# A token mixer with expert retrieval: the expert choice in finer steps, a block's last LayerNorm moved into the choice's empty steps

## The chip, the cores and the metric

The kernel runs on one core of one Trainium2 chip. Its time is the device time of one execution in microseconds (us). Five engines work side by side: TensorE (PE, matrix products), VectorE (DVE), ScalarE (ACT), GpSimd (POOL) and SyncE (SP), which only issues transfers. Each runs its own instructions strictly in order and waits for the others by semaphores.

## The reference

One layer over 128 context tokens and 512 latent tokens, 640 rows of 2048 float32 values. A token mixer (state-space scan, short convolution, Conformer convolution, gates) comes first, then the part that matters here, a retrieval among 16384 one-neuron experts:

- queries `q = h @ w_q` in 8 heads of two halves; each half is scored against 128 keys
- the 16 best of the 128 scores in each of the 16 columns (8 heads, two halves), then the 16 best of the 256 sums of pairs in each head: 128 experts for a token, with softmax weights `g`
- `out = sum over chosen experts k of g_k * gelu(x . u_k) * v_k`
- `y = LN(2 ** 0.25 * x1 + gate * out) * ln2_g + ln2_b`

## The kernel before

The 640 rows are five blocks of 128 tokens, taken in the order 3, 4, 2, 1, 0. Mixer, queries and scores of all blocks are done by 2530 us; the choice of the first block is done on the way. Then `experts` (L1374) runs to the end, half of the time.

**A block's experts.** For a block the union of its chosen experts is a list. `chunk` (L1265) treats 256 of its entries (134 chunks in all five blocks): GpSimd gathers the rows of `u` and `v` and of the weights (`ur`, `vr`, `gr`), PE transposes `u` (`turn`), ScalarE takes its high part `wh` and VectorE the low part `wl`, PE makes three products for each (`up`), then `weigh` and `down` add to four PSUM banks `acc`. 24 chunks (`K0`) are written out for each block, the few more stand behind conditions. `chunk` is a generator: it yields nine times, one yield a step. The first step holds two turns, the second `weigh`, and the third to eighth a turn each.

**What is dealt into the steps.** `choose` (L1034) for the next block is a generator too, and the caller asks it for one piece in every step. Its pieces, before the change:

- the 16 columns, two in a step (8 steps); the sums of pairs (2); the 8 heads, one in a step (8); splitting the places (1); one-hot sums that look up the experts' numbers (12); softmax (2): 33 steps
- a loop over n from 0 to 33 that makes the weights of all 16384 experts by one-hot products of four tokens on PE, two steps each for 32 of them. ScalarE copies a product into the staging tile `Gs`, which has one buffer; at n = 9, 17, 25 and 33 it is full and SP stores its 2 MB to `G_d`, in runs of 32 values. Four steps of counting on VectorE follow each time, and 20 empty steps behind the first three
- the list of the chosen experts: counts (1 step), 16 rounds of maximum and replacement, four in a step (4), places and reads of the first entries on GpSimd (9)

`finish` (L1302) of the block before, for blocks 1 to 3 of the order beside the choice, for block 4 alone: in chunk 0 it loads the rows of `x` and the gate and multiplies the four banks (`fy`); from chunk 1 on one piece in every second step: four of update and statistics, the square root, the row loads (`row`, L1339, four buffers), four of two updates each that take two LayerNorm rows of 512 values, and the store of the output. The last block's finish runs behind all chunks.

**The order of the work.** `pin` (L1359) ties every engine's instructions of one block's written-out part to the order in which they are written, SP's transfers too. SP issues ahead of the other engines as far as buffers are free.

Of the kernel before, what the change touches and what calls it, by code (L numbers as in the profile page):

```python
# [151 lines left out]
class Kern:  # L152
# [871 lines left out]
                self.nc.vector.scalar_tensor_tensor(x[:, s], x[:, s], a, g, op0=o0, op1=o1)  # L1024

    def top16(self, vals, idx, src):
        v = self.nc.vector
        v.max(vals[:, 0:8], src)
        v.max_index(idx[:, 0:8], vals[:, 0:8], src)
        v.match_replace(src, vals[:, 0:8], src, -3.0e38)  # L1030
        v.max(vals[:, 8:16], src)
        v.max_index(idx[:, 8:16], vals[:, 8:16], src)

    def choose(self, b, S=None):  # L1034
# [8 lines left out]
        IX = T.tile([128, 16, 16], U32, name="IX", tag="IX", bufs=1)  # L1043
        for c in range(16):
            self.top16(V[:, c], IX[:, c], S[:, c])
            if c % 2:
                yield
        IF = T.tile([128, 16, 16], F32, name="IF", tag="IF", bufs=1)
        v.tensor_copy(IF, IX)
        sh = [128, 8, 16, 16]  # L1050
# [3 lines left out]
        cand = T.tile(sh, F32, name="cand", tag="Gs", bufs=1)  # L1054
# [4 lines left out]
        TV = T.tile([128, 8, 16], F32, name="TV", tag="TV", bufs=1)  # L1059
        SE = T.tile([128, 8, 16], U32, name="SE", tag="SE", bufs=1)  # L1060
        for h in range(8):
            self.top16(TV[:, h], SE[:, h], cand[:, h].rearrange("p a b -> p (a b)"))
            yield

        I12 = T.tile([128, 3, 128], F32, name="I12", tag="I12", bufs=1)
# [30 lines left out]
        p = ps.tile([128, 3, 128], F32, name="g", tag="m", bufs=1)  # L1096
# [5 lines left out]
        for n in range(34):  # L1102
            if full is not None:
                n1, p = full
                if n1 % 8 == 0:
                    st = T.tile([128, 128, 32], F32, name="Gs", tag="Gs", bufs=1)
                nc.scalar.copy(st[:, :, n1 % 8 * 4:n1 % 8 * 4 + 4], p.rearrange("j t i -> j i t"))
                if n1 % 8 == 7:
                    nc.sync.dma_start(self.G_d[b][:NE].rearrange("(i j) t -> j i t", j=128)
                                      [:, :, n1 // 8 * 32:n1 // 8 * 32 + 32], st)  # L1110
            full = None
            if ready is not None:
                n1, oh, dd = ready
                p = ps.tile([128, 4, 128], F32, name="g", tag="m", bufs=1)
                for j in range(4):
                    nc.tensor.matmul(p[:, j], oh[:, j], dd[:, j], start=True, stop=True)  # L1116
                full = n1, p
            ready = None
            if n < 32:
                oh = T.tile([128, 4, 128], F32, name="oh", tag="oa", bufs=2)  # L1120
                dd = T.tile([128, 4, 128], F32, name="dd", tag="od", bufs=2)
                for j in range(4):
                    k1, k2, w = (it[:, i, n * 4 + j:n * 4 + j + 1] for i in range(3))
                    v.tensor_scalar(oh[:, j], self.iota, k2, None, op0=ALU.is_equal)
                    v.tensor_scalar(dd[:, j], self.iota, k1, w, op0=ALU.is_equal, op1=ALU.mult)
                    if j == 1:
                        yield
                ready = n, oh, dd
            yield
            if n % 8 == 1 and n > 1:  # L1130
                for q in range(4):
                    v.tensor_reduce(cnt[:, n // 8 - 1, q * 32:q * 32 + 32], st[:, q * 32:q * 32 + 32], axis=AX.X,
                                    op=ALU.add)
                    yield

                for _ in range(20 if n < 32 else 0):
                    yield

        f = T.tile([128, 128], F32, name="f", tag="f", bufs=1)
        v.tensor_reduce(f, cnt.rearrange("p q i -> p i q"), axis=AX.X, op=ALU.add)  # L1140
# [7 lines left out]
        for r in range(16):  # L1148
            s = slice(r * 8, r * 8 + 8)
            v.max(L[:, s], f)  # L1150
            if r < 15:
                v.match_replace(f, L[:, s], f, 0.0)
            if r % 4 == 3:
                yield
        li = T.tile([128, 128], I32, name="li", tag="li", bufs=1)
        v.tensor_scalar(li, L, -1.0, None, op0=ALU.add)
# [19 lines left out]
        p = ps.tile([128, 128], F32, name="g", tag="m", bufs=1)  # L1176
# [4 lines left out]
        p = ps.tile([128, 128], F32, name="g", tag="m", bufs=1)  # L1181
# [4 lines left out]
        p = ps.tile([128, 128], F32, name="g", tag="m", bufs=1)  # L1186
# [187 lines left out]
    def experts(self):  # L1374
        nc, tc = self.nc, self.tc
        E = self.E = self.pool("experts")
        one = lambda shape, name, dt=F32: E.tile(shape, dt, name=name)
        self.vr = [one([128, D], "vr%d" % j) for j in range(2)]
        self.y = one([128, D], "fy")
        self.t = one([128, CH], "t")  # L1380
        self.gr, self.w = one([128, 2, 128], "gr"), one([128, 2, 128], "w")
        self.ur = [[one([128, D], "ur%d%d" % (c, j)) for j in range(2)] for c in range(2)]
        hb = self.H[GB]
        self.xs = [[t[:, j] for t in hb] for j in range(2)]
        first = [one([128, D], "uf%d" % j) for j in range(2)]
        pieces = [[t[:, k * 512:k * 512 + 512]
                   for t in [self.wp.tile([128, 1024], F32R, name=n, tag=n, bufs=self.hl_bufs) for _ in range(3)]
                   for k in range(2)] for n in ("wh", "wl")]
        self.uh, self.ul = ([t.rearrange("p (k e) -> p k e", k=2) for t in p[:4]] for p in pieces)
        self.rr, self.nrow = [t.bitcast(F32) for p in pieces for t in p[4:]], 0  # L1390
        self.fx = [self.wp.tile([128, 1024], F32, name="wr", tag="wr", bufs=self.raw_bufs) for _ in range(2)]
        ps = self.pool("ps5", space=PSUM)
        self.acc = ps.tile([128, 4, 512], F32, name="acc")
        self.tb = [ps.tile([128, 512], F32, name="tb%d" % j) for j in range(2)]
        self.a = ps.tile([128, CH], F32, name="a")
        pending, rows, fin = None, None, iter(())
        mark = self.pin()
        self.load_x(0)
        for j in range(2):
            self.gather_u(self.order[0], 0, j)  # L1400
        for i, b in enumerate(self.order):
            more = self.choose(self.order[i + 1]) if i < 4 else iter(())
            for c in range(K0):
                if c == 0 and i:
                    fin = self.finish(i - 1)
                    next(fin)
                for n, _ in enumerate(self.chunk(i, c, pending, rows)):
                    next(more, None)
                    if c and n % 2:
                        next(fin, None)  # L1410
                if c == 0:
                    next(fin, None)
                rows, pending = None, (c == 0, self.xs[i % 2])
                if c == 0 and i < 4:
                    self.load_x(i + 1)
            for _ in more:
                pass
            if i < 4:
                rows = first
                for j in range(2):  # L1420
                    self.gather_u(self.order[i + 1], 0, j, first[j])
            n = nc.values_load(self.lists[b]["count"][0:1, 2:3].bitcast(I32), min_val=0, max_val=NE,
                               skip_runtime_bounds_check_because="it counts the ones among 16384 flags")
            self.pin(mark)
            pending = False, self.xs[i % 2]
            with contextlib.ExitStack() as st:  # L1426
                for c in range(K0, NCH):
                    st.enter_context(tc.If(n > c * CH, name="more%d_%d" % (i, c)))
                    mark = self.pin()
                    for _ in self.chunk(i, c, pending):  # L1430
                        pass
                    self.pin(mark)
            mark = self.pin()
        self.nbank = 1
        self.up(7, pending[1])
        self.weigh()
        for u in range(8):
            self.down(u, False)
        for _ in self.finish(4):
            pass  # L1440
        self.pin(mark)
        self.close(ps, E)
# [95 lines left out]
```

## Time and profile before

| | |
|---|---|
| median of three runs | 5276.44 us (5272.74 to 5280.17) |
| the profiled execution | 5268.44 us, its span 5266.7 us |
| PE busy | 4800.3 us, 91% of the span |
| VectorE busy | 2879.7 us, 55% |
| ScalarE, GpSimd busy | 1599.6 and 1601.8 us, 30% each |
| mean granted TensorE clock | 0.961 of full speed |
| moved by DMA | 1085 MB, mean 206 GB/s |

A share of busy time is a mean over stages with different limits, so the rows further below are cut by chunk: a chunk's limits are taken where VectorE's product of `weigh` (`w<-tb,gr`) starts, in its second step. SP issued a store at 3320.68 and the list `L_d` of the same block at 3514.48 us, two times that the text uses. A granted clock of 1.00 is the upper of TensorE's two levels, and a mean between the levels says how long it was at the lower one.

### The profile page before, as it was taken

What the parts mean: (1) busy time and instruction counts of PE and PEld (TensorE: products, weight loads), DVE (VectorE), ACT (ScalarE), POOL (GpSimd) and SP (SyncE); (2) the same over time, 40 slices, a digit from 0 to 9 for tenths busy, and PEclk for the clock granted to TensorE, in tenths of its full rate; (3) what the DMA queues carried; (4) which work ended last, traced back from release to release, by engine and by line L of the source; (5) the groups of instructions that cost most, each with busy time, mean ns of one, the idle gap of its engine ahead of it and who ended that gap; (6) DMA issues with size and microseconds to landing.
All of it is one profiled execution on the core that took longest, in us unless ns stands there. A gap on an engine that the chain in (4) does not pass through costs nothing. (4 is left out here: it accounts for less than half of the span.)

```text
span 5266.7 us, 74372 instructions
## 1 busy us (share of the span) xinstructions
PE 4800.3 (91%) x29015; PEld 3989.4 (76%) x29015; DVE 2879.7 (55%) x6240; ACT 1599.6 (30%) x2561; POOL 1601.8 (30%) x1628
## 2 busy tenths in 40 slices
PE   8999989999999997969699979997999889989997
PEld 3799879999999977759577657765677667767775
DVE  6693593466534544781555566555655484634333
ACT  3324424433223123323133223322332223323222
POOL 2000493000000004534243434343334434344442
PEclk8999989999999998989799999999999999999998
DMA  6544336554325465563578768776777668867765
GB/s 238 195 173 144 126 129 213 192 173 172 114 98 165 147 214 200 158 153 136 187 242 257 233 221 272 244 235 240 254 242 243 255 218 267 247 231 290 260 250 212
DMA packets 576711, 1085.00 MB, mean 206 GB/s; under 512 B 375643, under 2 KB 388955, under 8 KB 501819
## 3 DMA queue, kind: packets, MB, share of 16 engines
q0 software_dynamic: 97712, 596.41, 30.5%
q1 hardware_dynamic: 460394, 429.32, 27.4%
q10 hardware_dynamic: 18208, 54.08, 2.6%
q8 instruction: 239, 3.92, 0.3%
q14 instruction: 158, 1.29, 0.1%
HBM read 967.53 MB, written 112.13 MB: 205 GB/s over the span
## 5 line engine op out<-in xcount | busy, mean ns | idle before, releaser
L1241 DVE TENSOR_TENSOR wl<-tb,wh 128x512 fp32r<-128x512 f32 x1072 | 738.0, 690 | 1368.1 <-ACT wh L1240 1366.7
L1240 ACT CAST wh<-tb 128x512 fp32r<-128x512 f32 x1072 | 627.5, 585 | 1873.2 <-PE tb L1239 1776.6
L1262 PE MATMUL acc<-vr,w 128*128 128x512 f32 x2144 | 1096.8, 604 | 30.3 <-DVE w L1257 30.1
L1248 PE MATMUL a<-wh,hh 128*128 128x256 f32 x2144 | 966.9, 451 | 1.8 <-PEq L1426 1.8
L1239 PE MATMUL tb<-cst,ur 128*128 128x128 f32 x4160 | 649.6, 279 | 68.1 <-DMA ur<-in_pu,ix 58.1
L1248 PE MATMUL a<-wl,hh 128*128 128x256 f32 x2144 | 618.8, 289 | 48.9 <-DVE wl L1241 48.7
L193 ACT CAST wh<-wr 128x1024 fp32r<-128x1024 f32 x339 | 355.5, 1050 | 983.4 <-PE a L630 380.4
L1248 PE MATMUL a<-wh,hl 128*128 128x256 f32 x2144 | 614.2, 286 | 0.0
L1248 PEld LDWEIGHTS a<-wl,hh 128*128 128x128 f32 x2144 | 419.9, 196 | 255.3 <-issue 170.5
L1239 PEld LDWEIGHTS tb<-cst,ur 128*128 128x128 f32 x4160 | 493.1, 143 | 150.9 <-issue 75.8
L1248 PEld LDWEIGHTS a<-wh,hh 128*128 128x128 f32 x2144 | 420.4, 196 | 199.4 <-issue 189.7
L630 PE MATMUL a<-h,wl 128*128 128x320 f32 x2368 | 550.9, 313 | 19.4 <-DVE wl L194 19.4
L1204 POOL DMA_INDIRECT vr<-in_pv,ix x268 | 256.1, 955 | 1015.5 <-PE acc L1262 909.8
L194 DVE TENSOR_TENSOR wl<-wr,wh 128x1024 fp32r<-128x1024 f32 x281 | 343.8, 1225 | 380.3 <-ACT wh L193 373.6
L630 PE MATMUL a<-h,wh 128*128 128x320 f32 x2368 | 549.0, 313 | 0.0
L630 PE MATMUL a<-l,wh 128*128 128x320 f32 x2368 | 545.9, 312 | 0.0
L1262 PEld LDWEIGHTS acc<-vr,w 128*128 128x128 f32 x2144 | 341.4, 194 | 103.9 <-issue 69.2
L630 PEld LDWEIGHTS a<-h,wl 128*128 128x128 f32 x2368 | 400.9, 190 | 21.7 <-DVE wl L194 21.0
L1248 PEld LDWEIGHTS a<-wh,hl 128*128 128x128 f32 x2144 | 416.2, 194 | 0.0
L630 PEld LDWEIGHTS a<-h,wh 128*128 128x128 f32 x2368 | 405.6, 190 | 12.0
L630 PEld LDWEIGHTS a<-l,wh 128*128 128x128 f32 x2368 | 400.9, 190 | 0.8
L1204 POOL DMA_INDIRECT gr<-G_d,ix x268 | 265.9, 992 | 365.4 <-DVE w L1257 280.9
(396 smaller groups left out, 7450.0 us busy)
## 6 DMA issues: line engine op xcount, KB each, us to landing
wr<-in_wmod SPq DMA_DIRECT2D x152, 512.0 KB
wr<-in_win SPq DMA_DIRECT2D x83, 512.0 KB
G_d<-Gs SPq DMA_DIRECT2D x20, 2048.0 KB
wrx<-in_win SPq DMA_DIRECT2D x69, 512.0 KB
wrx<-in_wmod SPq DMA_DIRECT2D x40, 512.0 KB
wr<-in_wo SPq DMA_DIRECT2D x36, 512.0 KB
wr<-in_wq SPq DMA_DIRECT2D x32, 512.0 KB
wrx<-in_wq SPq DMA_DIRECT2D x32, 512.0 KB
```

The lines of the kernel that those rows point to most:

```text
L193: nc.scalar.copy(h, raw)
L194: (eng or nc.vector).tensor_sub(l, raw, h.bitcast(F32))
L630: nc.tensor.matmul(a, w, x[:, kt, c0:c0 + n], start=kt == 0 and i == 0, stop=kt == nk - 1 and i == 2)
L1204: self.nc.gpsimd.indirect_dma_start(out=out, out_offset=None, in_=table, in_offset=bass.IndirectOffsetOnAxis(ap=idx, axis=0))
L1239: nc.tensor.transpose(p[:, k, j * 128:j * 128 + 128], rows[j][:, kt * 128:(kt + 1) * 128], self.ident)
L1240: nc.scalar.copy(self.uh[g % 4], p)
L1241: nc.vector.tensor_sub(self.ul[g % 4], p, self.uh[g % 4].bitcast(F32))
L1248: self.nc.tensor.matmul(self.a, a[:, kt], w[:, k], start=kt + n == 0, stop=kt == 15 and n == 2)
L1262: self.nc.tensor.matmul(self.acc[:, d], self.w[:, j], self.vr[j][:, d * 512:d * 512 + 512], start=first and j == 0, stop=j == 1, skip_grou ...
```

## The change

`top16` is cut in two behind its replacement (`top16_steps`). The choice yields behind each column (16 steps for 8), twice in a head (16 for 8), and behind two rounds of the list in place of four (8 for 4). The empty steps behind a store are 13 in place of 20 and say so by yielding `"idle"`. The caller asks the finish for a piece only in a step in which the choice is idle or over, and no more in every second step; what might be left of it is drawn behind the chunks.

```diff
     def top16(self, vals, idx, src):
+        for _ in self.top16_steps(vals, idx, src):
+            pass
+
+    def top16_steps(self, vals, idx, src):
         v = self.nc.vector
         v.max(vals[:, 0:8], src)
         v.max_index(idx[:, 0:8], vals[:, 0:8], src)
         v.match_replace(src, vals[:, 0:8], src, -3.0e38)
+        yield
         v.max(vals[:, 8:16], src)
         v.max_index(idx[:, 8:16], vals[:, 8:16], src)
...
         for c in range(16):
             self.top16(V[:, c], IX[:, c], S[:, c])
-            if c % 2:
-                yield
+            yield
...
         for h in range(8):
-            self.top16(TV[:, h], SE[:, h], cand[:, h].rearrange("p a b -> p (a b)"))
+            yield from self.top16_steps(TV[:, h], SE[:, h], cand[:, h].rearrange("p a b -> p (a b)"))
             yield
...
-                for _ in range(20 if n < 32 else 0):
-                    yield
+                for _ in range(13 if n < 32 else 0):
+                    yield "idle"
...
-            if r % 4 == 3:
+            if r % 2:
                 yield
...
                 for n, _ in enumerate(self.chunk(i, c, pending, rows)):
-                    next(more, None)
-                    if c and n % 2:
+                    if next(more, "idle") == "idle" and c:
                         next(fin, None)
...
             for _ in more:
+                pass
+            for _ in fin:
                 pass
```

## Rows read from the trace of the kernel before

**Rows 1.** Busy us (instructions) by chunk: second block, ten undisturbed chunks.
```profile
core 0: us, PE busy (x) PEld busy (x) DVE busy (x) ACT busy (x) POOL busy (x), PEclk, DMA share, GB/s
3096.30:3130.30 34.00, 19.31 (x93) 13.27 (x94) 32.03 (x129) 4.48 (x8) 7.91 (x9) 0.90 0.55 196
3130.30:3160.30 30.00, 21.07 (x98) 14.48 (x97) 28.73 (x85) 6.35 (x10) 8.02 (x8) 0.84 0.44 152
3160.30:3182.00 21.70, 19.73 (x107) 14.73 (x106) 19.40 (x31) 6.34 (x11) 9.91 (x8) 0.89 0.55 178
3182.00:3203.30 21.30, 19.88 (x113) 14.84 (x111) 16.25 (x38) 8.65 (x14) 9.00 (x8) 0.93 0.90 322
...
3492.40:3514.60 22.20, 16.73 (x94) 12.22 (x95) 20.70 (x66) 4.79 (x9) 7.61 (x8) 0.96 1.14 321
3514.60:3535.30 20.70, 20.36 (x112) 15.60 (x111) 7.52 (x19) 5.40 (x11) 7.80 (x9) 0.88 0.48 164
3535.30:3557.40 22.10, 18.22 (x99) 13.92 (x98) 5.82 (x11) 5.07 (x9) 13.12 (x14) 0.92 0.59 223
...
4820.20:4990.20 170.00, 166.53 (x980) 123.99 (x980) 58.41 (x90) 50.66 (x90) 76.01 (x80) 1.00 0.69 255
```

**Rows 2.** The same: first block's chunks 0 to 3, last block's 1 to 3.
```profile
2561.50:2597.60 36.10, 20.11 (x88) 17.71 (x88) 33.70 (x142) 6.95 (x12) 1.26 (x2) 0.59 0.37 140
2597.60:2622.20 24.60, 19.21 (x100) 13.66 (x99) 23.46 (x77) 5.07 (x9) 7.60 (x8) 0.92 0.46 160
2622.20:2641.80 19.60, 18.94 (x105) 13.87 (x103) 16.15 (x19) 5.34 (x10) 9.35 (x8) 0.92 0.51 175
2641.80:2661.90 20.10, 18.40 (x111) 14.12 (x111) 13.70 (x34) 8.37 (x14) 8.81 (x8) 1.00 0.71 251
4750.40:4803.00 52.60, 50.64 (x300) 37.64 (x298) 29.15 (x52) 17.76 (x30) 23.60 (x24) 1.00 0.91 325
```

**Rows 3.** VectorE groups, chunk 0: count | busy us, mean ns | idle.
```profile
L1241 DVE TENSOR_TENSOR wl<-tb,wh 128x512 fp32r<-128x512 f32 x8 | 5.3, 674 | 0.0
...
L1030 DVE MATCH_REPLACE8 S<-V,S 128x128 f32<-128x128 f32 x14 | 3.9, 276 | 0.0
L1056 DVE TENSOR_TENSOR cand<-V 128x1024 f32<-128x1024 f32 x2 | 2.4, 1216 | 0.0
L1317 DVE TENSOR_TENSOR fy<-acc,wh 128x512 f32<-128x512 f32 x2 | 1.4, 683 | 0.0
L1030 DVE MATCH_VALUE_LOAD S<-V,S 128x8 f32 x14 | 1.3, 92 | 0.5
```

**Rows 4.** VectorE groups, chunk 1: a head's replacement.
```profile
L1030 DVE MATCH_REPLACE8 cand<-TV,cand 128x256 f32<-128x256 f32 x8 | 3.3, 408 | 0.0
```

**Rows 5.** GpSimd's timeline at the choice's end: start us, us, [idle before <-releaser].
```profile
3532.61 0.94 POOL L1204 DMA_INDIRECT vr<-in_pv,ix  x1 [5.93 <-PE acc L1262]
...
3547.68 0.95 POOL L1204 DMA_INDIRECT ur<-in_pu,ix  x1 [0.30 <-issue]
```

**Rows 6.** PE's waits from 3535.3 to 3557.4: us in total, times, longest.
```profile
PE tb L1239 <- DMA ur<-in_pu,ix: 3.9, 1, 3.9
```

**Rows 7.** SP's DMA queue (packets, MB), 2865 to 2893 and 3348 to 3354.5.
```profile
q1 hardware_dynamic: 16400, 2.10, 56.6%
...
q1 hardware_dynamic: 128, 0.02, 1.7%
```

**Rows 8.** Timelines: a store's issue on SP, ScalarE's next copy into `Gs`.
```profile
2865.00 0.36 SPq L1109 DMA_DIRECT2D G_d<-Gs  x1
...
2915.70 0.59 ACT L1107 COPY Gs<-g 128x512 f32<-128x512 f32 x1
```

**Rows 9.** DMA packets by size, 3514.6 to 3518.5, and 3518.5 to 3519.2.
```profile
DMA packets 313, 0.99 MB, mean 255 GB/s; under 512 B 65, under 2 KB 185, under 8 KB 214
...
DMA packets 33, 0.02 MB, mean 25 GB/s; under 512 B 22, under 2 KB 30, under 8 KB 33
```

**Rows 10.** SP's DMA queue, 3126 to 3133.4, four LayerNorm rows.
```profile
q1 hardware_dynamic: 576, 1.05, 49.5%
```

## The prediction, made before the changed kernel was run

> **What bounds the kernel now.** All that changes lies in the last stage, the experts: five blocks of 24 written-out chunks, nine steps each, with the choice for the next block and the finish of the last one dealt into those steps. I read first the busy time by chunk. Ten chunks without such work take 170.0 us, 17.0 each or 1.89 a step, with PE busy for 166.5 [rows 1]: there TensorE is the bound, with VectorE at 58.4, 5.84 a chunk. In the first two chunks of a block it is otherwise: 34.0 and 30.0 us, VectorE busy for 32.0 and 28.7, PE for 19 and 21 at a granted clock of 0.90 and 0.84 [rows 1]. The next two take 21.7 and 21.3, and three at the end of the choice 22.2, 20.7 and 22.1. The first block has no finish: 36.1, 24.6, 19.6, 20.1 [rows 2]. The chunks between carry the choice's one-hot products on PE; these are spread as before, and I count them as unchanged. Then I read VectorE's groups for the price of each step, GpSimd's timeline for the end of the choice, and the DMA queue for the store.
>
> **The choice's first part.** A column of the choice is five instructions of about 0.28 us and three loads of 0.09: 1.70 us [rows 3]. Before, two come in a step (3.4 us beside one low part, `wl`, of 0.67), after, one (2.4). A head is five of about 0.42 and three loads: 2.36 us [rows 4]; after, its steps hold 1.45 and 0.91. Counted from the second step of a chunk to that of the next, chunk 0 of a block has now 14 columns (23.8), the two sums of pairs with a cast (2.7), four products of the finish (2.7) [rows 3] and the chunk's own 5.84: 35.0, read 34.0, so neighbours overlap by 3%. After, it has 9 columns, 15.3 + 2.7 + 5.84 = 23.8, less 3%: 23.1. Chunk 1 has 6 columns, the sums and half a head, 10.2 + 2.7 + 1.45 + 5.84 = 20.2, less 3%: 19.6. Chunks 2 to 4 hold nine half heads or nine one-hot steps, which work on as many elements as the sums of pairs, 1.2 [rows 3]: some 10.5 + 5.84 = 16.3 at most: under PE's 17.0. What began in chunk 3 (softmax, first products) moves to chunk 5; without a finish beside it, it costs 3.1 over 17.0 [rows 2].
>
> Two engines that are both nearly full don't hide each other wholly: the first block's chunk 2 had 16.2 of VectorE and took 19.6, of which 8% is the clock (0.92, 1.6 us) and 1.0 is left [rows 2]. I add 0.5, 1.0, 0.7, 0.5 and 1.3 for chunks 0 to 4, 4.0 in all; the ends are none and 2.6 each, 13 a block. Over 17.0 the first chunks of blocks 1 to 3 cost 17.0 + 13.0 + 4.7 + 4.3 = 39.0 before and 6.1 + 2.6 + 4.0 + 3.1 = 15.8 after: 23 us saved in each, three times, 69. The first block saves 36.1 - 23.2 = 12.9 in chunk 0 (ten columns by the same count, clock 0.59 now), 24.6 - 20.6 = 4.0 in chunk 1, 1.9 in chunk 2, less 1.8 in chunks 3 and 4: 17.
>
> **The list's rounds.** Sixteen rounds of a maximum, a load and a replacement, three of a column's instructions on as many elements: 0.28 + 0.09 + 0.28 = 0.65 each [rows 3]. Four a step are 2.6 + 0.67 = 3.3 against PE's 1.89; two are 2.0. Four steps lose 1.4 each before, eight 0.1 after: 4.8 less. The next chunk's granted clock is 0.88 [rows 1], 2.5 us of 20.7; I count half of it back. 6 us a block, four blocks: 24; the ends are 2 and 9 a block.
>
> **Where the choice ends.** It has 189 steps now: 33 up to the products, 66 + 16 + 60 in them, 14 behind. After: 49, 66 + 16 + 39, 18: 188. So the six list reads on GpSimd come one step earlier, ahead of the chunk's last gather of `vr`. That gather waits for PE until 3532.61, the six come behind it, and by that `ur` for the next chunk but one is issued at 3547.68 [rows 5]; PE waits 3.9 for it [rows 6], in a chunk at clock 0.92. With the six in GpSimd's idle time before that gather, about 4 us of the backlog goes, and `vr` is not needed for half a chunk. 4 us a block, four blocks: 16; the ends are 0 (the reads are held by their own inputs) and 5.1, the chunk's whole excess.
>
> **The empty steps behind a store.** The staging tile has one buffer. A store's first overwriting copy came 26 steps after its issue, 2865.00 to 2915.70, 1.95 us a step [rows 8]; after the change 19 steps, some 37 us. That store's packets were all through within 28 us; the slowest, issued at 3320.68, had 128 of them behind 3348 and the last before 3354.5, at most 34 us [rows 7]. So the copy, behind which ScalarE's high parts are queued and for these PE, doesn't wait: 0, with 3 us to spare in the worst case.
>
> **The finish in the first empty stretch.** It leaves chunks 1 to 3 (counted above) and begins in the sixth step behind the first store: statistics in four steps, the square root, the row loads, four updates. Each of the eight adds two instructions of some 0.68, as the products of the finish take [rows 3], to one low part: 2.0 against 1.89. In block 4, where the finish runs alone in every second step, three chunks took 52.6, 1.6 over [rows 2]. In every step I take 2.5, three blocks: 7.5 lost, and 1.5 lost in block 4, which now deals it into consecutive steps; the ends are 0 and 5 each.
>
> Its LayerNorm rows are the new wait. In SP's order they now follow the store, and their first pair is wanted by VectorE twelve steps behind it, at 23.4 us. Do they pass the store? The list `L_d`, issued at 3514.48 while the fourth store was under way, shows it: 120 packets of 512 B to 2 KB by 3518.5, and the other 8 only then, with the store's last ones [rows 9]. So on each ring they stay behind: at 28 us, plus about a quarter of the 7.4 in which four such rows came [rows 10], less what runs on ahead on the other rings: I take 28.7. VectorE then stands for 5.3 us with the low parts queued behind the update, and PE has one step of work: 5.3 + 2.0 - 1.9 = 5.4, and about 2.1 for the clock (0.84 to 0.92 in starved chunks). 7.5 a block, three blocks: 22.5 lost; the ends are 0 and 14 each (a late ring, 34 us).
>
> The Trainium skill, in "DMA: Bandwidth & Descriptors", section "Queues, rings and completion order", speaks against this move: on each SDMA engine descriptors are consumed in ring order, and SP has one ring on each. By that rule the 22.5 are paid, and the trace agrees in the 8 late packets of the list; were rows free to pass the store, as on an idle queue, the sum would be 117 saved in place of 94.5.
>
> **Sum.** 17 + 69 + 24 + 16 - 7.5 - 1.5 - 22.5 = 94.5 us saved. The profiled execution took 5268.4, so 5174; the median of the three runs, 5276.4, is 8 above it, which gives 5182.
>
> **The rivals.** (a) The rows don't cost their wait: they land before 23.4 because most rings are early, or VectorE runs late by itself. For it: most of a store's packets go early; against it, an instruction needs all 128 packets. 5182 - 22.5 = 5160. (b) The evening out gives less: coupling at twice my 4.0 (16 us more over four blocks), the list reads held by their inputs (16), and a late ring in all three first stores (18): 5232. For it speaks chunk 2 of the first block, against it that the chunk started behind a full VectorE. (c) Slower than before: with 19 steps the store is not through, and ScalarE stands at twelve copies (three in each of four blocks). It decides from some 38.5 us on, 37 and one step of slack; to undo 94.5 each copy must stand 8 us, and with a store of 49 each stands 10.5: 5182 + 126 = 5308. Against it is the slowest store read, 34 us; for it only that gathers come denser once chunks are shorter. That the finish is not dealt as written can't well be: every empty step asks for it, and 11 pieces fit into 13.
>
> **Chances.** The forecast 0.52, (a) 0.20, (b) 0.22, (c) 0.06, of which 0.05 is slower. The range goes from 5140, (a) with no coupling at all (16 less) and a little more, to 5232, (b). A change under 0.2% (some 10 us, what a measurement of this kernel can tell) needs (b) and half of (c): 0.03. Faster 0.92.
>
> **What would show it.** Chunks 0 and 1 of blocks 1 to 3 at about 23.6 and 20.6 us, chunks 2 to 4 at 17 to 18.5; the chunk with the rounds at 17 to 18; no PE wait for `ur` near the end of the choice; a VectorE wait of some 5 us for a row of `in_lnr` in three blocks, once each; no wait of the staging copy for the store there. I am wrong if chunks 0 and 1 stay over 26 with VectorE not busy, if the copy waits for the store, or if the row wait is absent or above 12.

## The result: 79.8 us saved, 14.7 less than forecast

The changed kernel took 5195.95 us, the median of four runs (5186.60 to 5200.09), against 5275.76 for the kernel before on the same chip (5272.74 to 5280.17): a ratio of 0.9846, 95% interval 0.9829 to 0.9863. Forecast was 5182, in a range from 5140 to 5232. Its profiled execution took 5195.74 (span 5193.9), 72.7 below the profiled one of before. The medians lie 79.8 apart, since the one profiled before was 7.3 under the median beside which it stands here, the one after at it.

Busy time by chunk in the second block, cut as in [rows 1] (columns as there): chunks 0 to 2, then 7 to 9, then 19 and 21; the last row is the first block's chunk 0.

```profile
3071.60:3095.30 23.70, 18.81 (x96) 14.17 (x97) 21.77 (x85) 4.48 (x8) 8.55 (x9) 0.87 0.81 277
3095.30:3115.40 20.10, 18.92 (x102) 13.89 (x100) 18.53 (x67) 5.31 (x10) 7.80 (x8) 0.90 0.44 152
3115.40:3133.20 17.80, 16.96 (x98) 12.44 (x98) 15.01 (x45) 4.86 (x10) 7.61 (x8) 1.00 0.74 238
3211.70:3232.00 20.30, 19.60 (x124) 15.07 (x123) 14.92 (x34) 6.37 (x12) 7.65 (x8) 1.00 0.99 239
3232.00:3261.80 29.80, 16.96 (x95) 12.88 (x96) 15.82 (x31) 7.36 (x12) 7.85 (x8) 0.85 0.99 309
3261.80:3282.40 20.60, 19.38 (x119) 15.14 (x119) 11.91 (x33) 6.53 (x12) 7.94 (x8) 0.97 0.92 316
3459.30:3477.80 18.50, 16.69 (x98) 12.45 (x98) 14.93 (x58) 4.63 (x9) 7.60 (x8) 1.00 1.05 325
3495.80:3513.80 18.00, 16.88 (x100) 12.35 (x98) 5.83 (x10) 5.07 (x9) 10.45 (x11) 1.00 0.76 266
2566.40:2589.70 23.30, 15.06 (x91) 13.31 (x91) 21.77 (x91) 6.94 (x12) 1.03 (x2) 0.87 0.44 172
```

Chunks 0 and 1, 34.0 and 30.0 before [rows 1], take 23.7 and 20.1; the first block's chunk 0 falls from 36.1 [rows 2] to 23.3. Chunk 19, with the list's rounds, falls from 22.2 to 18.5 and VectorE's share of it from 20.7 to 14.9 us; chunk 21 takes 18.0, from 22.1. One chunk is new, 29.8 us with no engine busy for more than 17: the first one behind a store.

The waits in that chunk (in total, times, longest), and SP's own timeline there (start, duration):

```profile
PE tb L1260 <- DVE wl L1245: 12.4, 1, 12.4
...
DVE wr L1335 <- DMA wh<-in_lnr: 5.8, 1, 5.8
DVE wr L1336 <- DMA wl<-in_lnr: 3.9, 1, 3.9
...
DVE wr L1335 <- DMA wl<-in_lnr: 2.4, 1, 2.4
```

```profile
3218.86 0.37 SPq L1113 DMA_DIRECT2D G_d<-Gs  x1
3219.33 26.50 SPq L1348 DMA_DIRECT2D wh<-in_lnr  x1
3246.27 1.82 SPq L1348 DMA_DIRECT2D wl<-in_lnr  x2
3248.18 2.89 SPq L1348 DMA_DIRECT2D wh<-in_lnr  x2
```

VectorE stands three times for LayerNorm rows, 12.1 us together, with a low part queued behind; `weigh`'s transposes on PE wait 12.4 us for that, from 3247.6 to 3260.0. The granted clock falls to a mean of 0.85: some 9 of the 29.8 us at the lower level, 1.2 GHz. Most of these pass while PE stands; it worked at that level for only 3.2 us behind the wait:

```profile
3252.90:3260.00 7.10, 0.00 (x0) 0.00 (x0) 2.97 (x5) 0.00 (x0) 0.00 (x0) 0.50 0.76 295
3260.00:3263.20 3.20, 3.17 (x13) 2.96 (x14) 2.95 (x5) 0.33 (x1) 0.67 (x1) 0.50 0.91 219
```

The first row's issue alone stood 26.50 us on SP behind the store, until 3245.8; the others were issued only then. The store's packets ended at 3248.9. In the next two blocks the issue stood 22.95 and 22.47 us, and the chunk took 29.3 and 27.8.

One table shows where the time went. It sums the time of each chunk (from one start of `weigh`'s product to the next) over 17.0 us, by block in the order of work and by part of the choice: the first part (chunks 0 to 2 before, 0 to 4 after), the one-hot products (to chunk 18), the list (19 to 22), the rest of the block. Blocks are counted from one here and below; the prediction counts them from zero. Each pair is before, after:

| | first part | products | list | end of the block |
|---|---|---|---|---|
| 1st block | 29.3, 11.5 | 38.3, 39.3 | 13.8, 3.1 | 11.4, 9.2 |
| 2nd | 34.6, 12.9 | 38.5, 51.9 | 14.0, 3.5 | 11.6, 11.6 |
| 3rd | 34.0, 11.9 | 38.7, 53.0 | 13.5, 3.4 | 11.2, 9.0 |
| 4th | 34.0, 11.8 | 38.6, 54.1 | 13.9, 3.7 | 9.3, 11.5 |

The first part saves 83.8, the list 41.5, the products give back 44.2. The last block, which has no choice, loses 5.0, of which 2.6 in its first chunk. The stages ahead of the experts, which the change doesn't touch, took 4.9 us longer in this execution. In the traces of the eight runs below they took from nothing to 6 us longer than in the trace of before, so this is the spread from one execution to the next.

In the fourth block a third store, issued at 4432.0, was under way for 39.9 us instead of the 24.0 to 32.5 of the other stores beside the choice, and ScalarE's copy waited for it, the only such wait beside the experts in this trace:

```profile
ACT Gs L1111 <- DMA G_d<-Gs: 4.6, 1, 4.6
```

### The profile page after: what moved, and what is told of

Read it like the earlier page. It is cut to its first block, busy times and chain, and to the rows that moved or that the text cites. A ratio compares the mean times of both kernels' runs of the same rounds, so it can differ in the third digit from the quotient of the medians.

```text
span 5193.9 us, 74363 instructions
## 1 busy us (share of the span) xinstructions
PE 4766.5 (92%) x29015; PEld 3966.4 (76%) x29015; DVE 2875.1 (55%) x6240; ACT 1599.9 (31%) x2561; POOL 1591.8 (31%) x1628
## 3 DMA queue, kind: packets, MB, share of 16 engines
q0 software_dynamic: 97712, 596.41, 31.6%
## 5 line engine op out<-in xcount | busy, mean ns | idle before, releaser
L1252 PE MATMUL a<-wh,hh 128*128 128x256 f32 x2144 | 956.0, 446 | 1.8 <-PEq L1431 1.8
L630 PE MATMUL a<-h,wl 128*128 128x320 f32 x2368 | 550.6, 312 | 19.4 <-DVE wl L194 19.4
L630 PEld LDWEIGHTS a<-h,wl 128*128 128x128 f32 x2368 | 401.2, 190 | 21.6 <-DVE wl L194 21.0
L630 PEld LDWEIGHTS a<-h,wh 128*128 128x128 f32 x2368 | 405.3, 190 | 12.1
```

Of the source, the lines that this page charges most:

```text
L630: nc.tensor.matmul(a, w, x[:, kt, c0:c0 + n], start=kt == 0 and i == 0, stop=kt == nk - 1 and i == 2)
L1252: self.nc.tensor.matmul(self.a, a[:, kt], w[:, k], start=kt + n == 0, stop=kt == 15 and n == 2)
```

## The experiments

The eight runs were timed in two groups of four, each against the kernel before at a median of 5271.2 us. What a run saved is counted from there; the change as it stands ("after") saved 79.8 on its own chip. The edits are to the changed kernel where nothing else is said.

**The rows loaded ahead of the store.**

```diff
+        for j in range(2):   # behind the gate's products
+            nc.sync.dma_start(self.first[j], self.I["lnr"][2 + j:3 + j].to_broadcast([128, D]))
...
-            g = nxt
+            g = [self.first[j][:, s] for j in range(2)]
```

> The changed kernel, but the finish loads its LayerNorm rows (two whole rows of 2048 values, into the two tiles that hold the first rows of a block and are free after chunk 0) right behind the products with the gate, so ahead of the block's first store. Theory: what the move of the finish costs is the rows' wait behind the store (PE stood 12.4, 10.7 and 7.1 us in three blocks, and its clock was low for 10 to 14 us behind it). Then VectorE has no wait for rows there, the chunk of 27.8 to 29.9 us takes about 19, and the time is 5169 (5160 to 5178). Rival: the dense updates themselves make that chunk long; then it stays over 25 us and the time over 5188.

Measured 5152.32 (5147.29 to 5158.87), ratio 0.9774 [0.9761, 0.9787]: 118.9 us saved, 39 more than after and more than expected (5160 at best). Chunks 7 and 8 of the second block:

```profile
3210.50:3230.70 20.20, 19.54 (x124) 15.01 (x122) 14.83 (x33) 6.33 (x12) 7.65 (x8) 1.00 0.98 237
3230.70:3250.10 19.40, 17.01 (x98) 12.45 (x98) 15.91 (x31) 8.01 (x13) 7.86 (x8) 1.00 1.08 314
```

The chunk of 29.8 takes 19.4, with the same busy times on PE and VectorE and the clock at 1.00. No wait for a row is left on VectorE there. The products' column is 40.9, 42.8 and 41.0 in blocks 2 to 4: the rows' wait had cost 11.0, 10.2 and, with the copy's wait, 13.1. The finish by itself, beside the 38.5, 38.7 and 38.6 of before, costs 2.4, 4.1 and 2.4 there; but the first block, which has no finish, rises by 1.9 too. Read in the chunk behind the store alone, 19.4, 20.0 and 19.5 against 17.0, 17.2 and 17.0 with the finish dealt as before (below), it costs 2.4, 2.8 and 2.5. Of the 38.6 us between the spans of the two traces (5193.9 and 5155.3) 34 lie in that column; no copy waited in this run.

**Two quarters' rows issued by ScalarE's queue, at the same place.**

```diff
-        nxt = [row(self.I["lnr"][2 + j:3 + j, sl[0][1]]) for j in range(2)]
+        nxt = [row(self.I["lnr"][2 + j:3 + j, sl[0][1]], nc.scalar) for j in range(2)]
...                # quarter 1 the same; 2 and 3 stay on SP
```

> The changed kernel, but the first four row transfers of a finish (quarters 0 and 1) are issued by ScalarE on its own queue, the other four by SP as before. SP's first row transfer stood 26.5 us at issue behind the store. Theory: it is SP's queue alone that holds the rows, so on another queue they land in 3 to 5 us: VectorE's waits for them under 2 us each, some 15 to 25 us saved, 5171 to 5185. Rival: while a store of 16384 small runs is under way any queue's transfer stands at issue or is slow: then ScalarE stands for 10 us or more in three blocks with the high parts queued behind, and the time is 5205 or more.

Measured 5196.67 (5194.39 to 5201.80), ratio 0.9858 [0.9843, 0.9873]: 74.5 saved, no more than after. The expectation failed, and the rival's 5205 was not reached. The trace says why: ScalarE's timeline, then VectorE's wait.

```profile
3238.11 0.59 ACT L1244 CAST wh<-tb 128x512 fp32r<-128x512 f32 x1
3238.13 0.37 ACTq L1348 DMA_DIRECT2D wh<-in_lnr  x1
```

```profile
DVE wr L1335 <- DMA wh<-in_lnr: 9.1, 2, 6.0
```

The issue is not held here (0.37 us), but in ScalarE's order it comes behind the square root, at 3238.13, just before the row is wanted; the row then took 9.3 us. In the next two blocks it took 9.1, and in the last of them the store ended 2.0 us behind the issue. The run changed the queue but left no time between a row's issue and its use. So it didn't separate the queue from the store.

**The same two quarters on ScalarE's queue, in the finish's first empty step.**

```diff
+        ln = [[row(self.I["lnr"][2 + j:3 + j, sl[n][1]], nc.scalar) for j in range(2)] for n in range(2)]
         st = F.tile([128, 4, 6], F32, name="bst", tag="bst", bufs=1)
...
-        nxt = [row(self.I["lnr"][2 + j:3 + j, sl[0][1]]) for j in range(2)]
...                # quarters 2 and 3 are loaded by SP, two quarters ahead
```

> The change as it is, with the LayerNorm rows of quarters 0 and 1 issued by ScalarE's queue in the finish's first empty step, ahead of its statistics, some 12 us behind the store and some 12 us before they are wanted (the earlier run on ScalarE's queue issued them only at 22 us). Theory: what made the rows late is SP's queue, whose issue stood 26.5 us behind the store; on another queue a row takes about 9 us beside the store, so quarters 0 and 1 wait no more, and quarters 2 and 3 (still SP's) little: the long chunk falls from 28 to 30 to about 20 to 23, 5172 (5160 to 5184). Rival: beside a running store a row is slow on whatever queue (rings shared by all queues), lands at about 33 us again, and nothing is won: 5190 or more.

Measured 5188.83 (5180.89 to 5203.10), ratio 0.9846 [0.9832, 0.9859]: 82.3 saved. That misses the expected range and lies a little short of the rival's bound. The execution profiled was the slowest of the five, 14.3 us over the median. ScalarE's and SP's timeline, then VectorE's waits in the chunk, which took 31.1 us:

```profile
3230.42 0.37 ACTq L1348 DMA_DIRECT2D wh<-in_lnr  x1
```

```profile
3219.64 0.37 SPq L1113 DMA_DIRECT2D G_d<-Gs  x1
3245.62 11.59 SPq L1348 DMA_DIRECT2D wh<-in_lnr  x1
3257.65 0.81 SPq L1348 DMA_DIRECT2D wl<-in_lnr  x2
```

```profile
DVE wr L1335 <- DMA wh<-in_lnr: 8.8, 1, 8.8
...
DVE wr L1336 <- DMA wh<-in_lnr: 1.7, 1, 1.7
DVE wr L1336 <- DMA wl<-in_lnr: 1.6, 1, 1.6
```

Both halves of the theory hold and the sum is still no gain. On ScalarE's queue the rows issued 10.8 us behind the store pass it: in the last two of the three blocks quarters 0 and 1 waited not at all, in the first 1.7 us. On SP's queue the third quarter's row, asked for 26 us behind the store, still stood 11.59 us at its issue (5.51 and 8.08 in the other blocks), and the wait of 8.8 (8.5, 7.2) is its wait. And what passes a store delays it: the three stores were under way for 38.6, 38.6 and 37.3 us instead of 30.0, 31.2 and 24.0. The Trainium skill, "DMA: Bandwidth & Descriptors", section "Issuing engines are not separate DMA queues", says that DMAs of different engines interleave on the same 16 DMA engines, and that another issuer saves only its sequencer's issue time, usually small beside the DMA. The stores grown by 7.4 to 13.3 us agree; the small issue time doesn't: it was 0.37 us on one queue and 26.50 on the other.

**The finish dealt as before, the choice even.**

```diff
-                    if next(more, "idle") == "idle" and c:
+                    next(more, None)
+                    if c and n % 2:
                         next(fin, None)
```

> The changed kernel, but the finish is dealt as before the change: one piece in every second step from chunk 1 on. Theory: the evened steps carry the whole gain and the move of the finish is a loss as it stands. Chunk 1 of blocks 1 to 3 takes about 25 us (20 now), chunks 2 and 3 one to two more, the chunk with the waits 17.5 in place of 29, and block 4's chunks 1 to 3 5 us less: 5179 (5168 to 5190). Rival: the move carries a part of the gain, because chunks 1 to 3 can't take the finish beside the choice: 5205 or more.

Measured 5176.59 (5175.47 to 5178.86), ratio 0.9822 [0.9809, 0.9835], as expected. The second block's chunk 1 and its chunk behind the store:

```profile
3094.90:3119.30 24.40, 19.49 (x102) 13.60 (x100) 23.36 (x74) 6.35 (x10) 8.21 (x8) 0.92 0.53 182
3241.10:3258.10 17.00, 16.18 (x94) 12.02 (x94) 5.78 (x10) 4.79 (x9) 7.60 (x8) 1.00 1.09 320
```

The chunk behind the store takes 17.0, chunk 1 takes 24.4 in place of 20.1. So the evened choice alone gives 94.6 us (5271.2 to 5176.59). Moving the finish, as the change does it, costs 15 of these by the medians, though the intervals of the two ratios still overlap; with the rows ahead, the same move adds 24.3.

**Only the list's rounds evened, in the kernel before.**

```diff
-            if r % 4 == 3:
+            if r % 2:
                 yield
```

> The kernel before with one edit of the change alone: the list's sixteen rounds two a step in place of four; nothing else is evened out, the finish stays in every second step, and the reads of the list come four steps later than before. My prediction's term was 6 us a block for the rounds (4.8 at VectorE and half of the clock's 2.5 in the next chunk), 24 in four blocks: 5247 on this chip (5271 before). The reads that now come later may cost what the run with one more step cost (4.3 a block, 17 in all): then about 5264. Rival: the rounds were hidden beside the chunk's own slack, and the later reads cost: 5271 or more.

Measured 5244.48 (5238.98 to 5248.31), ratio 0.9950 [0.9937, 0.9964], as expected without a cost of the later reads. Chunks 19 to 22 of the second block:

```profile
3490.30:3508.60 18.30, 16.89 (x98) 12.47 (x98) 16.90 (x48) 5.23 (x10) 7.60 (x8) 1.00 1.13 312
3508.60:3526.50 17.90, 17.05 (x103) 13.02 (x104) 10.35 (x35) 4.97 (x11) 7.59 (x8) 1.00 0.78 273
3526.50:3543.70 17.20, 16.86 (x103) 12.74 (x102) 6.34 (x12) 5.07 (x9) 12.59 (x14) 1.00 0.53 189
3543.70:3564.80 21.10, 18.53 (x100) 13.50 (x98) 5.85 (x10) 5.06 (x9) 8.33 (x9) 0.92 0.70 252
```

26.7 saved. The list's column falls by 7.4, 7.5, 7.0 and 9.2 us, 31.1 in all; the stages ahead of the experts took 5.9 longer in this execution. The chunk with the rounds falls from 22.2 [rows 1] to 18.3, and the next to 17.9. The late chunk remains, 4.1 over 17.0 with the clock at 0.92, but one place later: the list reads now end in chunk 21, and the `vr` gathers behind them come late for chunk 22, where PE waits 2.2 us for one.

**One more step ahead of the list reads.**

```diff
         yield
+        yield
         for c in range(3):
```

> The changed kernel with one more empty step ahead of the six list reads at the end of the choice, which puts them behind the chunk's last gather of vr again, as before the change. Theory: their place in GpSimd's order is worth 4 to 5 us a block: the PE wait of 3.9 us for ur comes back in four blocks, 5214 (5208 to 5220). Rival: the wait went with the list's rounds, which no longer hold the gathers up: 5196 (5190 to 5202).

Measured 5213.46 (5209.26 to 5219.12), ratio 0.9891 [0.9876, 0.9906]: 57.7 saved, 22 fewer than after, as expected. The list's column shows 4.4, 5.1, 4.4 and 3.7 more, 17.6 in all; the last block took 4.5 more in this trace. PE's longest wait for `ur` in chunk 21, first here, then in after:

```profile
PE tb L1244 <- DMA ur<-in_pu,ix: 3.9, 1, 3.9
```

```profile
PE tb L1243 <- DMA ur<-in_pu,ix: 0.8, 1, 0.8
```

One step is enough to bring back the 3.9 of [rows 6]: the six reads come behind the last `vr`, and chunk 21 takes 22.5 again.

**Eight empty steps in place of thirteen, with the rows ahead.**

```diff
-                for _ in range(13 if n < 32 else 0):
+                for _ in range(8 if n < 32 else 0):
```

> The run with the LayerNorm rows loaded ahead of the store (5152), with eight empty steps behind a store in place of thirteen: 14 steps, some 27 us, from a store's issue to the first copy over its staging tile, where 19 steps made some 37. Theory: the stores read in the profile of after took 24 to 32.5 us and one 39.9, so that most of the copies now wait for their store, 0 to 6 us each; with twelve copies and half of each wait given back by the buffers ahead of PE, 5172 (5160 to 5195). The trace would show ScalarE's copy Gs waiting for the DMA G_d<-Gs in most of the 12 places. Rival: PE has enough queued, or the list that comes earlier pays for it: 5152 or less.

Measured 5191.76 (5189.63 to 5200.48), ratio 0.9857 [0.9842, 0.9872]: 39.4 lost against the rows ahead alone, twice the expected 20. ScalarE's waits over the four blocks:

```profile
ACT Gs L1111 <- DMA G_d<-Gs: 21.4, 8, 6.1
```

Eight of the twelve copies waited, 21.4 us together. A copy stops ScalarE's high parts with it: the chunk in which the third store was still under way took 29.7, 29.9 and 30.4 us in blocks 1 to 3, where the longest waits were about 6, and 21.8 in block 4, where none was over 1.0. So a wait of 6 cost some 8. The rest of the loss was not taken apart.

**The columns in half steps too, with the rows ahead.**

```diff
-            self.top16(V[:, c], IX[:, c], S[:, c])
+            yield from self.top16_steps(V[:, c], IX[:, c], S[:, c])
             yield
```

> The run with the rows ahead of the store (5152), with the sixteen columns dealt as thirty-two half steps too. Theory: chunks 0 and 1 are bound by VectorE as long as a step holds a whole column (23.6 and 20 us against 17.0); with halves the same work lies beside four chunks and fits under PE: about 6 us a block saved, the more so since PE's clock stays up; in four blocks 5127 (5115 to 5140). The list then comes at the 204th of 216 steps, 16 later. Rival: the later list costs as the run with one more step did (4.3 a block) or more, and nothing is won: 5150 or more.

Measured 5122.36 (5120.94 to 5127.46), ratio 0.9722 [0.9708, 0.9735]: 148.8 saved, the fastest, 30 us below the rows ahead alone. The second block's chunks 0 and 1:

```profile
3056.10:3077.40 21.30, 19.09 (x95) 13.90 (x96) 14.55 (x49) 4.48 (x8) 8.55 (x9) 0.84 0.71 265
3077.40:3096.50 19.10, 17.60 (x104) 12.72 (x102) 12.65 (x47) 5.18 (x10) 7.60 (x8) 1.00 0.98 376
```

VectorE's 21.8 and 18.5 in these chunks fall to 14.6 and 12.7. Chunk 0 still has a clock of 0.84 in this block and takes 21.3; in the next two blocks it takes 18.3, where it took 23.6 and 24.0 with the rows ahead alone. Chunk 1 hardly gains: 19.1, 19.9 and 19.8, where it took 19.7, 19.2 and 19.2 with VectorE busy for over 18. So something else holds it at that length; this was not taken apart. The first block's chunk 0 falls from 23.2 to 15.4, its block sum by 15.1; the others' by 4.1, 8.2 and 7.4. The list that comes later costs nothing: its six reads go ahead of chunk 22's last `vr`, that chunk and the next take 17.5 and 17.1, and the columns of products and list together hold 40.1 to 43.9 us (44.0 to 46.7 with the rows ahead alone).

## Why the prediction was right, and where its sum was off

*The choice's first part* (17 and three times 23): 17.8, and 21.7, 22.1 and 22.2. (Of each 23, 1.2 were for the softmax steps, which the table has among the products.) Chunk 0 was to take 23.6 and took 23.7, 23.6 and 23.6, chunk 1 20.6 and took 20.1, 19.2 and 19.2, chunks 2 to 4 17.8 to 18.1. Counting VectorE's instructions by step, less 3% for overlap, plus a small coupling came out near. That VectorE was the bound of chunk 0 is shown by the half columns, which take it lower still. For chunk 1 it is not shown: there the half columns took VectorE from 18.3 to 12.7 us, and the chunk stayed.

*The list's rounds and its reads* (6 and 4 a block, 40): 10.7, 10.5, 10.1 and 10.2, 41.5 in all. Taken apart, the rounds alone saved 26.7 us (31.1 in the list's column), and one more step ahead of the reads cost 17.6 in the list's column, 4.4 a block. Both mechanisms stand.

*The finish in the empty steps* (2.5 a block): 2.4, 2.8 and 2.5, read in the chunk behind the store with the rows ahead. The products' column gives 2.4, 4.1 and 2.4, but it moves by as much as 1.9 where there is no finish.

*The LayerNorm rows' wait* (7.5 a block, 22.5) is the term that was wrong, in size: 11.0, 10.2 and 10.2 (13.1 less the 2.9 that the copy's wait added to its chunk), 31. The first wait was as forecast, 5.8 us (5.3), at 31.1 us behind the store instead of 28.7 and wanted at 25.3 instead of 23.4. But I let the whole wait end with the first row. Behind it came further waits, 3.9 and 2.4 here (2.3, 1.3 and 1.2 in the next block; 3.0, 0.8 and 0.3 in the last), so that VectorE stood 12.1, 11.6 and 10.1 us. PE stood 12.4, 10.7 and 7.1 us for it (and 2.6 more in the last), where I had 5.4. The cause was not quite the one that I gave, either. I had the rows issued early and waiting on each ring, as the list `L_d` did [rows 9]. But `L_d` was issued 27 us behind its store, when 16378 of the store's 16400 packets had gone, in 0.33 us; the first LayerNorm row, 0.5 us behind a store, was held at its issue for 22 to 27 us, and the three others were not even issued until it was through. With my picture the four rows should have come nearly together. The clock's part was about right, 2.1 forecast: PE worked at the lower level for 3.2, 5.0 and 6.7 us behind its wait, and half of that is lost, 1.6, 2.5 and 3.4.

The trace of before had shown such a hold, in a stage whose SP timeline I hadn't read, where a weight is loaded 2.0 us behind a store of the first block's choice. That store's packets ended at 2289.1:

```profile
2272.30 0.37 SPq L1109 DMA_DIRECT2D G_d<-Gs  x1
2274.27 12.70 SPq L191 DMA_DIRECT2D wrx<-in_wo  x1
```

*The last block* (1.5): 5.0. With the finish in consecutive steps its rows come one quarter at a time, and VectorE waited 3.3 us for one in chunk 1, which took 21.0. The other 2.6 are in chunk 0, which as cut here now holds the finish's first piece, and whose clock was 0.85 instead of 0.91.

*The copy behind the store* (0): right for eleven of twelve. The twelfth had a store of 39.9 us, longer than the slowest that I had read, 34, and than the 38.5 from which I let rival (c) decide; its chunk took 2.9 us longer. It was no chance of one execution: in four of the eight runs (both with rows on ScalarE's queue, the finish dealt as before, the later reads) the same store took 36.9 to 37.3 us, and the copy waited 1.8 to 2.2. What made it long stays open: at the same place the run with the rows ahead had one of 31.6. That the mechanism of (c) is real, eight empty steps show.

So two of the prediction's own signs of being wrong came, each in one place: a copy waited for its store, and the row wait passed 12 us (12.1). The time is inside the range all the same, since the large terms held.

Of the rivals, (a) was the change without its row wait: 117 us saved by forecast, 118.9 measured once the wait was taken away by loading earlier. (b), an evening that gives less, is refuted by the first two items; of its third term, a late ring in all three first stores, 9 of 18 us came. The difference between the forecast 94.5 us and the 72.7 of the traces is, by item: 8.9 for the rows, 5.4 outside the blocks (4.9 ahead of them, 0.5 behind), 3.5 in the last block, 2.9 for the copy, 2.2 in the first part, 1.4 for the finish (by its column), 1.0 among the first block's products, less 2.2 at the blocks' ends and 1.5 more from the list: 21.6 of 21.8. The 4.9 lie within the spread of the traces; the 0.5 and the 2.2 touch nothing of the change, and whether they are chance wasn't tried.

## What to carry over

A step moved into an empty place brings its transfers with it: look up what their queue is doing at that place, look in the trace at hand for any issue that already stands there, and load ahead of the big store what will be wanted behind it. Price a wait for several transfers by the last one that comes, not by the first. And count the work of the busy engine step by step against the bound engine's step: where a step holds more than the other has time for, cutting it in two paid in each of the three runs that tried it, though not in each chunk.

## What was not expected of the hardware

An issue on SP's queue directly behind a store of 16384 pieces of 128 bytes stood 22.47 to 26.50 us; the issues on ScalarE's queue beside such a store took 0.33 to 0.82 us, and where VectorE waited for the first of these rows it was there 9.1 to 9.3 us later. In the changed kernel the hold ends ahead of the store's own end (3245.8 and 3248.9, 3763.3 and 3771.0, 4298.9 and 4299.9), when 16278, 16305 and 16136 of the 16400 packets had gone; where an issue was asked for 26 us behind the store, it still stood 5.51 to 11.59 us. Why the queue holds, its count of pieces or its bytes, was not tried.
